# From the first layer to attention in one list of steps, with the query latent's inverse root moved into the exponential

## The chip, the cores and the metric

The kernel runs on one core of a Trainium2 chip. The metric is device microseconds of one execution, lower is better. Times of the profile are from one execution under the hardware profiler.

## The reference

Two layers over 1024 tokens of width 1024, all in 32-bit floats. Layer 0 is a short gated convolution and a squared-ReLU MLP. After it a shared key and value side is built from the residual stream, and layer 1 is attention over it, with an MLP. What concerns the change:

```python
hkv = modulate(rmsnorm(x, kv_norm_g), shift, scale)
kv_a = hkv @ kv_a_w                                    # 256 latent columns, 64 rotary ones
c_kv = rmsnorm(kv_a[..., :KV_LORA], kv_a_norm_g)
k_pe = apply_rope(kv_a[..., KV_LORA:], cos, sin)
kv = (c_kv @ kv_b_w).reshape(B, S, N_HEADS, QK_NOPE + V_HEAD)
...
q = (rmsnorm(h @ q_a_w, q_a_norm_g) @ q_b_w).reshape(B, S, N_HEADS, QK_NOPE + QK_ROPE)
# 8 heads; 384 latent columns; q_nope (128 wide) and rotated q_pe (64), both times 1/sqrt(192)
s = q_nope . k_nope + q_pe . k_pe;  masked block-causally in chunks of 64
p = softmax(s);  o = p @ v
```

## The kernel before

Each product of two matrices is made of three TensorE matmuls (`mm`, L170): both operands are split into a high and a low part, and low x high, high x low and high x high are summed in PSUM. The high part is a copy on ScalarE (the engine rows name it ACT), the low part a subtraction on VectorE (DVE) of the high part from the source; for weights that is `split_w`, L173 and L174. Most of the 512-column matmuls of a trace are such products.

Tokens are held in 8 tiles of 128 rows, or in 2 halves of 512. A framework schedules the instructions on each engine; where the code says `pinned()`, the written order is kept as it stands. Tiles on chip come from pools with a fixed number of buffers: `mm` and `tp` are PSUM banks of 512 columns, `big` ones of 1024; two `big` ones exist. `raw_tile()` gives one of four buffers for data from memory, and the transfers into them are queued in order on SyncE (SP).

The **end of layer 0's MLP** makes 24 matmuls for each of the 8 token tiles. `Seam` follows each with the sum, a norm, the gated residual and the norm for what comes next: on VectorE L309, L315, L316, on ScalarE two passes with squares (L255), a root (L257), and the row that the transposes need (L295). `h_steps` makes transposed operands for half the tokens: a group of four 128x128 transposes for each of 8 column blocks (L484), a scaled copy on ScalarE (L486, `tt`), and the split on VectorE (L490, L491). `first_block` then makes the first three column blocks of the query latent for half 0, with those steps between.

`latent` does, for the query latent (3 blocks) and the key-value latent (2), for each half: a copy from PSUM (L1305), squares (L1306), a sum over partitions by a matmul with ones (L1309), a root (L1310), a reciprocal over 128x512 elements (L1311), the scaling (L1313), and the split (L1314, L1315). `rotary_keys` makes the rotary keys: four copies of 32 partitions on ScalarE (L1322), and products with a cosine table `ctab` and a sine table `stab` on VectorE (L1323 to L1325).

**Attention** starts with `queries` (L1424, L1425), `rotary` and `keys` (L1418, L1419) of head 0, for half 1 and then half 0. Each head works through 8 score tiles from the longest (1024 keys) to the shortest: `scores` makes the matmuls into a `big` buffer (L1465), sets the masked corner (L1466), takes the negated maximum (L1468), the exponential with that maximum as bias and a running sum (L1471), and, as `end`, the reciprocal and the normalisation (L1475, L1476). `turn` transposes the weights p (L1491) and splits them (L1494, L1495), and the products with the values follow. Values of two heads at a time are made by `values` (L1448, L1449). Between them stand background tasks, sums of conditioning weights on VectorE (L195), whose weights come by 512 KB transfers. `load_q_b` and `load_kv_b` fetch the weights of the next heads.

Of the kernel before, what the change touches and what calls it, by code (L numbers as in the profile page):

```python
# [12 lines left out]
ALU = mybir.AluOpType  # L13
# [20 lines left out]
MASKED = -(2.0 ** 127)  # L34
# [17 lines left out]
P5_3 p6_0 nt2d p4_1 p3_2 D9_3 nS2 p6_3 nS3 p7_3 ns2a o6 p4_3 nt3a ns2d p5_3 nt3d o5 o4 p3_3 o3 o7  # L52
""".split()
# [8 lines left out]
def trunk_kernel(ctx: ExitStack, tc: tile.TileContext, x, c, ada_w, ada_b, norm_g, conv_in_w, conv_w,  # L62
# [95 lines left out]
    nc.vector.memset(eps_1, EPS)  # L158
    nc.scalar.activation(small(), eps_1, AF.Sqrt)
# [315 lines left out]
    def h_steps(tp, ys, half, key, dst):  # L475

        hi, lo = dst
        s1, sh = vtile["s" + key], vtile["h" + key]
        tts = {}

        def step(k):
            p_ = tp_ps()
            for t in range(4):
                nc.tensor.transpose(p_[:, t * P:(t + 1) * P], ys[half * 4 + t][:, k * P:(k + 1) * P], ident)  # L484
            tt = tp.tile([P, HALF], F32, tag="tt", name=nm("tt"), bufs=2)
            nc.scalar.activation(tt, p_, AF.Identity, scale=s1[:, k:k + 1], bias=sh[:, k:k + 1])  # L486
            tts[k] = tt

        def split(k):
            nc.vector.tensor_copy(hi[:, k, :], tts[k])  # L490
            nc.vector.tensor_tensor(lo[:, k, :], tts[k], hi[:, k, :].bitcast(F32), op=ALU.subtract)  # L491

        return [(lambda k=k: step(k), lambda k=k: split(k)) for k in range(KD)]

# [130 lines left out]

    def first_block(seam, steps0, steps1, ws, h):

        ps_ = [mm_ps(), mm_ps(), big_ps()[:, :HALF]]
        for k in range(KD):
            with pinned():  # L630
                for p_, w in zip(ps_, ws):
                    mm(p_, (w[0][:, k, :], w[1][:, k, :]), (h[0][:, k, :], h[1][:, k, :]), k == 0, k == KD - 1)
                if k == 0:
                    seam.back()
                    seam.front(steps0, 2)
                    seam.flush()
                elif k == 1:
                    seam.back()
                elif k >= 4:
                    seam.back()  # L640
                    seam.front(steps1, 2)
        with pinned():
            seam.back()
        return ps_
# [647 lines left out]
    def halves_of(*tiles):  # L1292
        return [t_[:, i * HALF:(i + 1) * HALF] for t_ in tiles for i in range(2)]
# [376 lines left out]
```

## Time and profile before

| | |
|---|---|
| time, median of 3 runs | 2152.4 us (2151.09 to 2154.95) |
| profiled execution | 2151.04 us, span 2149.3 us |
| TensorE busy (PE) | 2083.8 us, 97% |
| its weight loads (PEld) | 1712.5 us, 80% |
| VectorE (DVE) | 1530.3 us, 71% |
| ScalarE (ACT) | 1060.0 us, 49% |

The span is what the trace covers of the execution; a few microseconds lie around it. A row of the timeline gives start, duration, engine, line, operation, output and input, and in brackets the idle time ahead of it with what ended it. A row of the groups gives busy microseconds and mean nanoseconds of one, then the idle time ahead. A row of the windows gives for a stretch its length, the busy time of PE, PEld, DVE, ACT and POOL with counts, the granted TensorE clock, the share of the DMA engines, and GB/s.

### The profile page before, as it was taken

How to read it: one execution, taken by the hardware profiler on the slowest of the kernel's cores; microseconds unless marked ns; L12 is line 12 of the kernel's file. 1: busy time of each engine (PE TensorE's matmuls, PEld its weight loads, DVE VectorE, ACT ScalarE, POOL GpSimd, SP SyncE). 2: the span in 40 equal slices, each digit the busy share in tenths (PEclk: the TensorE clock that was granted, in tenths of full speed). 3: DMA queues.
4: the chain of work that ended last, by engine and by line, in shares of the span. 5: the costliest groups of instructions: out<-in, count | busy, mean ns of one | idle time of the engine just before them, and what ended most of it. 6: DMA issues, size and time to landing. Idle time of an engine off the chain costs nothing.

```text
span 2149.3 us, 25252 instructions
## 1 busy us (share of the span) xinstructions
PE 2083.8 (97%) x9638; PEld 1712.5 (80%) x9638; DVE 1530.3 (71%) x2063; ACT 1060.0 (49%) x1512; POOL 4.0 (0%) x8
## 2 busy tenths in 40 slices
PE   6999999999999999999899999999999999999998
PEld 5888888888888778888677888877888887788887
DVE  5877776977665677956788877765976665558556
ACT  4633354845454534344665555564845543444342
POOL 0000000000000000000000000000000000000000
PEclk9999999999999999999999999999999999999999
DMA  8344464466443976444214231043455543853243
GB/s 244 99 145 143 136 205 135 131 200 210 152 144 127 324 268 240 167 147 167 86 55 129 78 107 42 25 162 126 132 187 186 172 162 130 293 191 125 98 147 137
DMA packets 242335, 330.85 MB, mean 154 GB/s; under 512 B 18629, under 2 KB 143906, under 8 KB 242214
## 3 DMA queue, kind: packets, MB, share of 16 engines
q1 hardware_dynamic: 204328, 248.57, 36.6%
q10 hardware_dynamic: 37886, 80.67, 9.9%
q8 instruction: 76, 1.25, 0.2%
q14 instruction: 45, 0.37, 0.1%
HBM read 248.45 MB, written 80.74 MB: 153 GB/s over the span
## 4 chain that ended last, share of the span: by engine, by line
PE 73%; DVE 12%; ACT 7%; DMA 5%; issue 2%; SPq 0%; ACTq 0%; DVEq 0%
PE one L170 38%; PE mm L170 19%; PE tp L170 6%; PE big L170 4%; ACT junk L255 2%; DMA raw<-in_ada_w_dram 2%; PE big L1465 2%; DVE y L315 1%; DVE raw L316 1%; DVE acc L195 1%; PE tp L1491 1%; DMA raw<-in_kv_ada_w_dram 1%; DVE ring L174 1%; ACT small L257 1%; DVE y L309 1%
## 5 line engine op out<-in xcount | busy, mean ns | idle before, releaser
L170 PE MATMUL one<-slot,uphi 128*128 128x512 f32 x1240 | 382.0, 389 | 0.0
L170 PEld LDWEIGHTS one<-slot,uphi 128*128 128x128 f32 x1240 | 232.8, 188 | 48.5 <-issue 0.5
L170 PE MATMUL big<-slot 128*128 128x512 f32 x1152 | 265.6, 390 | 1.1 <-DVE slot L174 0.6
L170 PEld LDWEIGHTS big<-slot 128*128 128x128 f32 x1152 | 215.3, 188 | 47.0 <-DVE y L919 1.1
L170 PE MATMUL one<-slot,uplo 128*128 128x512 f32 x620 | 243.5, 393 | 3.6 <-ACT y L581 2.1
L170 PE MATMUL one<-ring,ring 128*128 128x512 f32 x1008 | 232.3, 391 | 6.2 <-DVE ring L174 6.1
L173 ACT ACTIVATE ring<-w 128x1024 fp32r<-128x1024 f32 x98 | 103.7, 1058 | 263.5 <-PE tp L170 134.0
L170 PEld LDWEIGHTS one<-ring,ring 128*128 128x128 f32 x1008 | 188.2, 188 | 49.2 <-ACT ring L173 5.6
L174 DVE TENSOR_TENSOR ring<-w,ring 128x1024 fp32r<-128x1024 f32 x98 | 119.9, 1223 | 111.5 <-ACT ring L173 111.5
L174 DVE TENSOR_TENSOR uplo<-raw,uphi 128x1024 fp32r<-128x1024 f32 x117 | 142.8, 1223 | 79.0 <-ACT uphi L173 78.9
L173 ACT ACTIVATE uphi<-raw 128x1024 fp32r<-128x1024 f32 x117 | 123.7, 1059 | 135.6 <-PE one L170 76.9
L170 PE MATMUL mm<-ring,ring 128*128 128x512 f32 x672 | 162.7, 390 | 1.0 <-DVE ring L174 1.0
L170 PE MATMUL tp<-ring,ring 128*128 128x512 f32 x672 | 161.7, 389 | 0.0
L170 PE MATMUL mm<-slot,uphi 128*128 128x512 f32 x504 | 158.3, 395 | 0.4 <-DVE slot L430 0.4
L170 PEld LDWEIGHTS mm<-ring,ring 128*128 128x128 f32 x672 | 125.6, 188 | 28.5 <-DVE ring L174 2.0
L170 PEld LDWEIGHTS tp<-ring,ring 128*128 128x128 f32 x672 | 126.1, 188 | 26.2
L195 DVE SCALAR_TENSOR_TENSOR acc<-raw,csil,acc 128x1024 f32<-128x1024 f32 x88 | 112.6, 1279 | 40.3 <-DMA raw<-in_ada_w_dram 36.0
L170 PEld LDWEIGHTS one<-slot,uplo 128*128 128x128 f32 x620 | 116.4, 188 | 30.3 <-ACT y L581 3.8
L174 DVE TENSOR_TENSOR ring<-raw,ring 128x1024 fp32r<-128x1024 f32 x98 | 119.6, 1220 | 18.1 <-ACT ring L173 18.1
L170 PE MATMUL one<-slot,s 128*128 128x512 f32 x468 | 112.6, 389 | 0.6 <-DVE s L174 0.6
L170 PEld LDWEIGHTS mm<-slot,uphi 128*128 128x128 f32 x504 | 94.8, 189 | 21.1 <-issue 1.4
L581 ACT ACTIVATE y<-one 128x512 f32<-128x512 f32 x62 | 36.7, 592 | 142.8 <-PE one L170 98.5
(271 smaller groups left out, 3486.5 us busy)
## 6 DMA issues: line engine op xcount, KB each, us to landing
ha<-y ACTq DMA_DIRECT2D x196, 256.0 KB, 3.0
raw<-ha SPq DMA_DIRECT2D x98, 512.0 KB, 4.1
raw<-in_ada_w_dram SPq DMA_DIRECT2D x80, 512.0 KB, 4.4
raw<-in_mlp_up_w_dram SPq DMA_DIRECT2D x70, 512.0 KB, 5.0
w<-in_mlp_down_w_dram SPq DMA_DIRECT2D x56, 512.0 KB, 4.9
raw<-hd SPq DMA_DIRECT2D x24, 512.0 KB, 4.5
xs<-raw ACTq DMA_DIRECT2D x24, 512.0 KB, 3.0
raw<-xs SPq DMA_DIRECT2D x24, 512.0 KB, 4.1
```

Source lines behind the costliest of these rows:

```text
L170: nc.tensor.matmul(out_, lhs[a], rhs[b], start=first and i == 0, stop=last and i == 2, skip_group_check=more)
L173: nc.scalar.activation(hi, src, AF.Copy)
L174: nc.vector.tensor_tensor(lo, src, hi.bitcast(F32), op=ALU.subtract)
L195: nc.vector.scalar_tensor_tensor(acc, raw, s, acc, op0=ALU.mult, op1=ALU.add)
L255: nc.scalar.activation(junk, src, AF.Square, accum_out=ss)
L257: nc.scalar.activation(rt, ss, AF.Sqrt, bias=eps_d)
L309: nc.vector.tensor_tensor(y, y, p_, op=ALU.add)
L315: nc.vector.scalar_tensor_tensor(y, y, rroot(ss), self.gmb, op0=ALU.mult, op1=ALU.mult)
L316: nc.vector.tensor_tensor(xr, xr, y, op=ALU.add)
L581: nc.scalar.activation(dst, x_, AF.Copy)
L1465: nc.tensor.matmul(o_, a, m_, start=j == 0, stop=j == 4)
L1491: nc.tensor.transpose(p_[:, c:c + P], pts[4 * hf + i][:, j * P:(j + 1) * P], ident)
```

## The change

There are three parts.

1. A list of step names, `LATENTS`, replaces `h_steps`, `first_block`, `latent` and `rotary_keys`. From token tile 5 on, everything from the MLP's end to the last kv latent is written in that order, all pinned. Its names: `mm5` products of tile 5; `tr0_2`, `tu0_2`, `sp0_2` transposes, scaled copy and split of column block 2 for the queries' half 0 (`k0`, `k1` for the keys'); `f0` to `f7` and `g0` to `g3`, `e0` to `e2` the query latent's products; `qh`, `ql`, `qq` its high part, low part and squares; `qs`, `qr`, `qi` sums, root and inverse; `v..` the same for the kv latent; `k..` the rotary keys; `wa`, `wd` the split of the kv weights.
2. The query latent is not normalised any more. Its parts are taken from PSUM with the gain as the only factor. The sum of squares goes, by four matmuls of one column for each half, into a table `rsq` of 128x8, one column for each query tile, with the softmax's 1/sqrt(192) folded in. Each score tile multiplies its negated maximum by its column (one 128x1 operation on VectorE), and the exponential takes it as its scale. The mask's value becomes -2^120.
3. At attention's start the order becomes queries and rotary of half 1, keys of half 0, values 0 and 1, queries and rotary of half 0, keys of half 1. Values 2 stand after score tile 7, values 3 after tile 6 (both stood after 6 before). Five background tasks a head are called in heads 1 to 6 in place of 0 to 5.

```diff
-MASKED = -(2.0 ** 127)
+MASKED = -(2.0 ** 120)
+LATENTS = """
+mm5 tr0_0 mm6 tu0_0 add5 sp0_0 sq5 rc4 pre4 stt5 tr0_1 xad5 tr0_2 tu0_1 mm7 add6 dma5 tu0_2 sp0_1 sqx5 sp0_2 sq6 rc5
...
+vh11 vh10 vl11 vl10 ks1 kh1 kl1
+""".split()
...
-        down(slots, sizes, wd, src_fn, ys, seam, steps0, 0, lambda: ws.extend(up_weights(up, [w]) for w in wcols), begun)
+        down(slots, sizes, wd, src_fn, ys, seam, None, 0, lambda: ws.extend(up_weights(up, [w]) for w in wcols), begun)
...
-            nc.scalar.activation(raws[m], p_, AF.Copy)
-            nc.scalar.activation(sqs[min(m, 1)], raws[m], AF.Square)
...
-        nc.tensor.matmul(sp, ones, sqs[0], start=True, stop=True)
-        nc.scalar.activation(rs, sp, AF.Sqrt, scale=1.0 / (n * P), bias=eps_1)
-        nc.vector.reciprocal(rs, rs)
-        for m in range(n):
-            nc.vector.scalar_tensor_tensor(raws[m], raws[m], g[:, m:m + 1], rs, op0=ALU.mult, op1=ALU.mult)
-            nc.scalar.activation(dst[0][:, m, sl], raws[m], AF.Copy)
...
+        def q_high(hf, m):
+            nc.scalar.activation(qaT[0][:, m, half(hf)], out_[hf][m], AF.Copy, scale=gq[:, m:m + 1])
...
+        def q_sums(hf):
+            p_ = t_["qs", hf] = big_ps() if hf else mm_ps()
+            for t in range(4):
+                nc.tensor.matmul(p_[:, t:t + 1], t_["sq", hf][0][:, t * P:(t + 1) * P], ones[:, 0:1], start=True, stop=True)
...
+        def q_root(hf):
+            nc.scalar.activation(rsq[:, 4 * hf:4 * hf + 4], t_["qs", hf][:, :4], AF.Sqrt, scale=(NOPE + ROPE) / QL, bias=eps_q)
...
+        with pinned():
+            for name in LATENTS:
+                acts[name]()
...
+        rs = rsq[:, i:i + 1]
+        nc.vector.tensor_tensor(mx, mx, rs, op=ALU.mult)
...
-        nc.scalar.activation(pt, sp[:, :n], AF.Exp, bias=mx, accum_out=l_)
+        nc.scalar.activation(pt, sp[:, :n], AF.Exp, scale=rs, bias=mx, accum_out=l_)
...
-    for hf in (1, 0):
-        queries(Q, qw_, hf)
-        rotary(R, qw_, hf, tp_ps)
-        keys(K, kw, 0, hf)
+    queries(Q, qw_, 1)
+    rotary(R, qw_, 1, tp_ps)
+    keys(K, kw, 0, 0)
+    for b in range(2):
+        values(V, kw, b)
+    queries(Q, qw_, 0)
+    rotary(R, qw_, 0, tp_ps)
+    keys(K, kw, 0, 1)
...
-        run_bg(5)
+        run_bg(5 if h else 0)
...
-            values(V, kw0, 0)
-            values(V, kw0, 1)
+            values(V, kw0, 2)
...
-            values(V, kw0, 2)
             values(V, kw0, 3)
```

How the instructions stand on the engines, in three places. First TensorE at the end of the MLP. Each run of four rows with `big` is one token tile's products; `tp` is a group of transposes and `y` a tile's row. Before:

```order
L170 MATMUL big_7479<-slot_7214 128x512 x6
L484 MATMUL tp_7515<-cs,y_5382 128x128
L484 MATMUL tp_7515<-cs,y_5383 128x128
L484 MATMUL tp_7515<-cs,y_5384 128x128
L170 MATMUL big_7539<-slot_6957 128x512 x6
L170 MATMUL big_7539<-slot_6958 128x512 x6
L170 MATMUL big_7539<-slot_6959 128x512 x6
L170 MATMUL big_7539<-slot_7214 128x512
L484 MATMUL tp_7515<-cs,y_5385 128x128
```

And in the changed kernel:

```order
L187 MATMUL big_7507<-slot_7217 128x512 x6
L1318 MATMUL tp_7532<-cs,y_5385 128x128
L1318 MATMUL tp_7532<-cs,y_5386 128x128
L1318 MATMUL tp_7532<-cs,y_5387 128x128
L1318 MATMUL tp_7532<-cs,y_5388 128x128
L187 MATMUL big_7537<-slot_6960 128x512 x6
L187 MATMUL big_7537<-slot_6961 128x512 x6
```

The fourth transpose of the first group, the one of tile 3's row, stood after 19 of the 24 products of tile 6 and now stands ahead of them all.

Second, ScalarE at the start of attention. `kw` is the high part of the kv weights for heads 2 and 3, `z` the rotary copies of the queries, `k` the keys, `r` the rotated queries, `v` the values. Before:

```order
L1322 ACTIVATE z_8376<-tp_8377 32x512 x4
L1348 ACTIVATE slot_6957<-y_8314 128x512
L1418 ACTIVATE k_8407<-mm_8400 128x512
L1424 ACTIVATE q_8421<-mm_8411 128x512
L1434 ACTIVATE r_8394<-z_8375 64x512
L1434 ACTIVATE r_8395<-z_8375 64x512
L1322 ACTIVATE z_8426<-tp_8427 32x512 x4
L1418 ACTIVATE k_8457<-mm_8450 128x512
L1448 ACTIVATE v_8510<-mm_8497 128x512
L1434 ACTIVATE r_8444<-z_8425 64x512
L1434 ACTIVATE r_8445<-z_8425 64x512
L173 ACTIVATE kw_8953<-raw_8831 128x1024
```

And in the changed kernel:

```order
L1534 ACTIVATE q_8362<-mm_8352 128x512
L190 ACTIVATE kw_8937<-raw_8813 128x1024
L1269 ACTIVATE z_8367<-tp_8368 32x512 x4
L1528 ACTIVATE k_8398<-mm_8391 128x512
L1422 ACTIVATE ckT_7227<-y_8255 128x512 x2
L1558 ACTIVATE v_8415<-mm_8402 128x512
L1445 ACTIVATE slot_6960<-y_8322 128x512
L1544 ACTIVATE r_8385<-z_8366 64x512
```

`kw`, which stood behind the rotary copies, keys and r's of both halves, now stands ahead of those of the first.

Third, VectorE in head 0's score tiles. `small` with `big` as its source is a tile's maximum, `p` the exponentials, `acc` a background task. Before:

```order
L1475 RECIPROCAL small_8529<-small_8495 128x1
L1468 TENSOR_REDUCE small_8544<-big_8532 128x1
L1476 TENSOR_SCALAR p_8494<-p_8494,small_8529 128x1024
L1449 TENSOR_TENSOR v_8562<-mm_8549,v_8562 128x512
L1449 TENSOR_TENSOR v_8578<-mm_8565,v_8578 128x512
```

And in the changed kernel:

```order
L1587 RECIPROCAL small_8520<-small_8502 128x1
L1578 TENSOR_REDUCE small_8535<-big_8523 128x1
L1588 TENSOR_SCALAR p_8501<-p_8501,small_8520 128x1024
L1580 TENSOR_TENSOR small_8535<-small_8535,rsq 128x1
L1576 MEMSET big_8560 64x64
```

The new 128x1 product stands behind the normalisation of the tile before, and the exponential needs it; before, the exponential needed the maximum alone.

More of the change, by code (lines that the diff above doesn't have):

```diff
@@ L473, in quarter_steps @@
         return acts
[L475 to L493, printed above, removed]
     def up_weights(up, cols, kk=KD):
@@ L624, in up_mm @@
         return p_
[L626 to L644, printed above, removed]
     def first_pairs(seam, acts, up, wmat, ws, ops):
```

231 lines of the change are left out of this document (171 added, 60 removed).

## The prediction

> **What bounds the kernel now.** I read the page first, then windows of 25 us over the stretch that the change rewrites (1010 to 1165 us), then TensorE's timeline there with its waits, and last the rows that price single operations.
>
> ```profile
> span 2149.3 us, 25252 instructions
> PE 2083.8 (97%) x9638; PEld 1712.5 (80%) x9638; DVE 1530.3 (71%) x2063; ACT 1060.0 (49%) x1512; POOL 4.0 (0%) x8
> PE 73%; DVE 12%; ACT 7%; DMA 5%; issue 2%; SPq 0%; ACTq 0%; DVEq 0%
> ```
>
> TensorE is busy for 97% of the span. Only 2149.3 - 2083.8 = 65 us are there to be won by order alone. The windows (columns: PE busy, PEld, DVE, ACT, POOL, then granted TensorE clock) show that the stretch holds some of them:
>
> ```profile
> 1025.00:1050.00 25.00, 20.50 (x100) 16.21 (x99) 18.90 (x32) 16.34 (x27) 0.00 (x0) 0.93 0.32 106
> 1050.00:1075.00 25.00, 22.85 (x116) 18.20 (x115) 20.05 (x29) 16.08 (x25) 0.00 (x0) 1.00 0.22 62
> 1075.00:1100.00 25.00, 25.00 (x130) 19.43 (x129) 21.19 (x33) 14.96 (x23) 0.00 (x0) 1.00 0.10 26
> 1125.00:1150.00 25.00, 21.05 (x112) 16.90 (x111) 24.30 (x37) 16.58 (x27) 0.00 (x0) 1.00 0.58 180
> ```
>
> Idle are 4.50 us at the end of the MLP (and the clock falls), 2.15 after it, nothing in the middle, 3.95 where attention starts; there VectorE is full (24.30 of 25). The timeline of TensorE names the waits in brackets:
>
> ```profile
> 1031.18 1.33 PE L484 MATMUL tp<-cs,y 128*128 128x128 f32 x8 [3.41 <-ACT tt L486]
> 1056.22 0.48 PE L170 MATMUL mm<-slot,uplo 128*128 128x512 f32 x1
> 1070.66 0.50 PE L170 MATMUL mm<-slot,uplo 128*128 128x512 f32 x1 [2.03 <-ACT lat L1305]
> 1071.46 0.60 PE L484 MATMUL tp<-cs,y 128*128 128x128 f32 x4
> 1071.82 0.47 PE L170 MATMUL mm<-slot,uplo 128*128 128x512 f32 x1
> 1120.25 2.20 PE L170 MATMUL mm<-slot,w 128*128 128x512 f32 x9
> 1122.29 2.20 PE L170 MATMUL tp<-slot,w 128*128 128x512 f32 x9
> 1157.38 1.09 PE L1491 MATMUL tp<-cs,p 128*128 128x128 f32 x8 [0.37 <-DVE p L1476]
> 1158.72 0.50 PE L170 MATMUL mm<-pt,v 128*128 128x512 f32 x1 [0.25 <-ACT pt L1494]
> ...
> 1028.00:1031.00 3.00, 0.00 (x0) 0.00 (x0) 2.90 (x7) 2.85 (x5) 0.00 (x0) 1.00 0.23 91
> 1033.00:1036.00 3.00, 3.00 (x8) 2.04 (x7) 2.90 (x8) 2.82 (x7) 0.00 (x0) 0.53 0.75 265
> ```
>
> Nine matmuls take 1122.29 - 1120.25 = 2.04 us, 0.227 each. After the idle 3.41 us the clock fell to 0.53 and the nine of the next block took 3.9, so 1.85 more; after the idle 2.03 (in the window from 1050) it stayed at 1.00. A group of four transposes takes 1071.82 - 1071.46 = 0.36.
>
> **The change part by part.** First, the end of the MLP. In the new order TensorE's tile 6 stands behind the first whole group of four transposes, and the fourth of them needs tile 3's row, which ScalarE writes here:
>
> ```profile
> 1017.05 1.14 ACT L295 ACTIVATE y<-raw,small 128x1024 f32<-128x1024 f32 x1
> 1014.30 1.06 ACT L255 ACTIVATE junk<-raw 128x1024 bf16<-128x1024 f32 x1 [2.14 <-DVE raw L316]
> 1020.32 1.06 ACT L255 ACTIVATE junk<-raw 128x1024 bf16<-128x1024 f32 x1 [2.14 <-DVE raw L316]
> 1014.63 0.49 PE L484 MATMUL tp<-cs,y 128*128 128x128 f32 x3
> ```
>
> The row is there at 1018.2; the first three, which need older rows, are done by about 1015.0 (1014.63 and 0.36). So a new wait of 3.2 us arises. It costs little as such: ScalarE and VectorE pass a tile in 1020.32 - 1014.30 = 6.02 us, TensorE needs 24 x 0.227 = 5.45, so it must wait for them in any case. Walking on, two tiles at 5.45 and two transpose groups bring the last product to about 1030.0; eight blocks of 2.04, five transpose groups (0.36) and one wait, about 1.35 by the same rows, for the last operand that VectorE splits end at 1050.4; seven groups of the next half, which the kernel before does among its blocks, make it 1052.9. The same work stands at 1056.22 now: **-3.3 us**. The new wait of 3.2 lies between 2.03 (clock kept) and 3.41 (clock lost) and nearer to the latter, so I charge the lost clock: 1.85, of which two tiles' slack of 0.57 each takes 1.15, so +0.7. **-2.6** in all; bounds -3.3, and 0 if the wait is only moved.
>
> The Trainium skill ("TensorE: Matmul & The Clock Gate", section "HAM oscillation — how this bites in real kernels") gives about 3.4 us of idleness, a free-running window, as what halves the clock. By that 3.2 would not do it and this term would be 0.7 lower; that an idle 3.41, just one window long, did it here says that the edge is not sharp, so the row stands.
>
> Second, the q latent. Its normalisation leaves the way (the wait of 2.03 hangs on it), and two sums over partitions change their form:
>
> ```profile
> L1309 PE MATMUL tp<-sq,ones 128*128 128x512 f32 x8 | 4.5, 641 | 0.2
> L214 PE MATMUL one<-ones,acc 128*128 128x1 f32 x32 | 3.7, 245 | 0.0
> L1311 DVE RECIPROCAL sq<-sq 128x512 f32<-128x512 f32 x4 | 13.4, 3351 | 5.9 <-ACT sq L1310 5.9
> ```
>
> Eight records for four sums are 2 x 0.641 = 1.28 us for each; four columns of one are about 4 x 0.23. Two sums: 2 x (1.28 - 0.92) = 0.7 saved; the wait of 2.03 goes, since queries' raw sums now go from PSUM straight to operands. Two reciprocals of 3.35 leave VectorE, which had no wait of TensorE under them in the full window (1075 to 1100), so they pay nothing themselves. **-2.7 us**; -0.7 if another wait takes that one's place. So the first query product (1120.25) starts 5.3 earlier, at T = 1114.9.
>
> Third, the start of attention. ScalarE's high part of the kv weights for heads 2 and 3 now stands ahead of the rotary copies of the first half. Before, it stood behind the second pair of r's and waited for nothing:
>
> ```profile
> 1132.63 1.44 SPq L127 DMA_DIRECT2D raw<-in_q_b_w_dram  x3
> 1135.38 0.37 SPq L127 DMA_DIRECT2D raw<-in_kv_b_w_dram  x1
> 1139.10 1.06 ACT L173 ACTIVATE kw<-raw 128x1024 fp32r<-128x1024 f32 x1
> 1125.23 2.39 ACT L1322 ACTIVATE z<-tp 32x512 f32<-32x512 f32 x4
> 1128.31 0.60 ACT L1418 ACTIVATE k<-mm 128x512 fp32r<-128x512 f32 x1
> 1128.92 0.68 DVE L1324 TENSOR_TENSOR z<-z,stab 128x512 f32<-128x512 f32 x1
> 1129.53 0.68 DVE L1419 TENSOR_TENSOR k<-mm,k 128x512 fp32r<-128x512 f32 x1
> raw<-in_q_b_w_dram SPq DMA_DIRECT2D x4, 192.0 KB, 2.6
> ```
>
> Its transfer is on SP's queue behind three for q weights, whose buffer was the sine table's until VectorE's last multiplication with it. That one ends at about T + 2.5 (four copies of 2.39 in all after the rotary key product, then two VectorE operations). The q requests take 1.44, so the kv request goes at T + 3.9 at the earliest; landing takes between 2.6 (the smaller q transfer) and 3.72 (1139.10 - 1135.38), I take 3.2: T + 7.1. ScalarE gets there at T + 3.0 (the key product is done one sum over partitions, 1.2, before T, its four copies end at T + 1.2, then come three operations of some 0.6) and stands for 4.1 us. Behind it in its queue: 1.06 for itself, four rotary copies (2.39), keys' copy (0.60), two halves of the kv latent (about 0.60 each); behind those on VectorE the rotary product, two low halves, an addition, the sine product and the keys' low part, at 0.61 each (1129.53 - 1128.92): T + 14.8. For that one TensorE's second block of values waits, as it reuses keys' PSUM buffer; TensorE is there after 33 x 0.227 + 12 x 0.12 = 8.9. It waits **5.9 us**. Carried on by the same rows: values, now ahead of the scores, no longer lie under the softmax, so score tiles 4, 3 and 2 wait 1.4, 1.6 and 1.8 us for an exponential, and the last score block before the transposes ends at T + 40.9. Now that is 1157.38 - 1120.25 = 37.13. **+3.8 us**; without the blocked queue it would be -0.1, the lower bound, and the 2.3 us by which the rows of before exceed products plus waits could come on top: +6.1. An idle 5.9 loses the clock (3.41 did): 1.85, of which the two short waits right behind it (0.4 and 0.9) hide 1.3: **+0.5**. Next, score tile 1 waits about 1.15 where the wait at 1158.72 is 0.25: **+0.9**.
>
> Fourth, every score tile gets one more VectorE operation of 128x1 between the maximum and the exponential, and the exponential reads one more operand of one value per partition:
>
> ```profile
> L219 DVE TENSOR_TENSOR v<-v,vecs 128x8 f32<-128x8 f32 x4 | 0.6, 158 | 0.0
> L1476 DVE TENSOR_SCALAR p<-p,small 128x640 f32<-128x640 f32 x7 | 3.9, 552 | 0.2
> L1305 ACT ACTIVATE lat<-mm 128x512 f32<-128x512 f32 x8 | 4.5, 594 | 2.5 <-DVE ckT L1315 1.2 <-PE mm L170 0.7 <-DVE slot L1315 0.6
> L486 ACT ACTIVATE tt<-tp,v,v 128x512 f32<-128x512 f32 x32 | 23.9, 774 | 12.0 <-PE tp L484 11.0 <-DVE slot L491 0.6 <-PE mm L170 0.3
> PE tp L1491 <- DVE p L1476: 1.2, 4, 0.3
> PE big L1465 <- ACT p L1471: 1.1, 2, 0.7
> ```
>
> The operation is bounded by the nearest row, 0.16 us for 128x8 (0.15 taken). A copy from PSUM takes 594 ns, one with two such operands 774, so each is 0.09. So 0.24 us more per tile, 64 times; VectorE, busy for 71% of the span, has room for 64 x 0.15 = 9.6. In addition the order puts an operation between the maximum and the new one in most tiles, in half of them the normalisation of the tile before, 0.55 by the middle row; together about 0.7. What hides this: two score tiles have PSUM room, and TensorE has the last head's transposes and products to do meanwhile. The waits of TensorE on this chain in heads 1 to 7 (1165 to 1410 us, the last two rows: us, times, longest) are six, and each grows by 0.24 at least: **+1.4 us**; with the other operation in each, 6 x 0.7 = 4.2; nothing, if slack elsewhere takes it. The plain folds (scale of 1/sqrt(192), the mask's value, the sine table) exchange operations of equal length: nothing, under VectorE's other work. Of the five running sums of conditioning weights that move from head 0 to head 6, head 0's VectorE keeps as many in the new order, and head 6 has VectorE time free: nothing; without that cover five operations of at most twice the 0.68 of a row half as wide, 6.8.
>
> Sum: -2.6 - 2.7 + 3.8 + 0.5 + 0.9 + 1.4 = **+1.3 us**. The profiled execution took 2151.04 (span 2149.3), so 2152.3 in its terms; the runs' median is 2152.4, 1.4 above it, so I forecast **2153.7 us**. A measurement of this kernel can tell about 0.2%, 4.3 us, from no change: I forecast no change.
>
> **The rivals.** *The transfer comes in time, and the softmax stays covered.* For it: 3.2 us for landing and the request's time are my bounds' middle, and in heads 1 to 7 TensorE waits for this chain six times only. Then the 5.9 shrinks by the blocked 4.1 less 0.2, the clock holds, and score tile 1 and the heads lose nothing: 2153.7 - 3.9 - 0.5 - 0.9 - 1.4 = 2147.0, faster. Against it: SP's queue is in order, and the sine buffer's release fixes the request.
>
> *The softmax chain comes out from under TensorE's work* and the kernel is slower. Place: score tiles of all heads, TensorE's wait for the exponential. Price 0.7 per exposed tile, 56 tiles in heads 1 to 7. It decides from the point where a quarter of them is exposed: 14 x 0.7 = 9.8, less the 1.4 counted: 2153.7 + 8.4 = 2162.1. For it: half of the tiles wait behind a normalisation. Against it: only six waits on the chain there now, none above 0.7.
>
> *The change doesn't do what it says at the MLP's end:* the wait of 3.41 is only moved to the first transpose group and delays all behind it. The first term is 0 instead of -2.6: 2156.3. For it: the new wait is nearly as long. Against it: ScalarE and VectorE set the pace there.
>
> **How the numbers follow.** Forecast 0.43, transfer in time 0.36, softmax exposed 0.16, wait moved 0.05. The forecast's own spread (its bounds on the sums, some 3 us either way, 2150 to 2158) puts 0.04 of it on faster, 0.70 on same, 0.26 on slower. The second case is faster in three of four, the third slower in nearly all, the last half same, half slower. Faster 0.017 + 0.27 = 0.29; same 0.30 + 0.09 + 0.02 = 0.41; slower 0.11 + 0.16 + 0.03 = 0.30. The range reaches just past the two outer cases' prices, 2146 to 2162.
>
> **What would show it.** Right: in the new profile the first transpose group carries a wait near 3.2 and the idle 2.03 for the latent's copy is gone; the first query product starts near 1115; ScalarE's high part for kv waits some 4 us for its transfer there, and TensorE stands near 6 us before the second values block, with the clock at half after it. Wrong: if that copy waits for no transfer, the second case holds; if heads 1 to 7 show TensorE waiting on exponentials more than some ten times, the third; if the first query product does not start before 1119, the last. The forecast as a whole is wrong outside 2148.1 to 2156.7.

## The result and the profile after

The changed kernel takes 2166.53 us (median of four runs, 2163.71 to 2169.63) against 2151.9 for the kernel before beside it: ratio 1.0066, interval [1.005, 1.0082]. By the ratio it is slower by 14.2 us, and its time lies outside the range of 2146 to 2162. Its profiled execution has a span 14.5 us longer. From its page, the span, the busy time of the engines, and the chain's shares:

```profile
span 2163.8 us, 25317 instructions
PE 2097.1 (97%) x9650; PEld 1716.8 (79%) x9650; DVE 1523.2 (70%) x2122; ACT 1061.8 (49%) x1506; POOL 4.0 (0%) x8
PE 80%; DVE 8%; ACT 6%; DMA 4%; issue 1%; ACTq 0%; SPq 0%; DVEq 0%
```

TensorE is busy 13.3 us longer (2083.8 before) though its records count only twelve matmuls more. Nearly the whole loss looks like work, not like waiting; that is the first thing to explain. Its windows over the rewritten stretch (the columns are those of the prediction):

```profile
1025.00:1050.00 25.00, 25.00 (x126) 20.93 (x125) 18.50 (x32) 19.70 (x34) 0.00 (x0) 0.98 0.63 188
1050.00:1075.00 25.00, 25.00 (x136) 20.90 (x136) 15.90 (x29) 13.80 (x21) 0.00 (x0) 1.00 0.01 3
1075.00:1100.00 25.00, 23.39 (x131) 19.78 (x130) 20.55 (x37) 16.54 (x26) 0.95 (x1) 1.00 0.16 46
1125.00:1150.00 25.00, 22.33 (x118) 18.09 (x117) 24.65 (x36) 16.96 (x28) 0.00 (x0) 1.00 0.29 88
```

TensorE's idle time there is 1.6 us in the third window and 2.7 in the last; the 4.5 and 2.15 of the kernel before in the first two are gone (a new wait of 3.04 stands just ahead of them, in the rows below). To see where time goes I cut the execution at four places that both kernels have: the first transposes behind the MLP's tile 5, the first query product, the first and the last transposes of p, and TensorE's end. Rows of TensorE's timeline, changed kernel:

```profile
1018.92 0.49 PE L1318 MATMUL tp<-cs,y 128*128 128x128 f32 x3
1022.45 0.48 PE L1318 MATMUL tp<-cs,y 128*128 128x128 f32 x1 [3.04 <-ACT y L312]
1120.40 2.62 PE L187 MATMUL mm<-slot,w 128*128 128x512 f32 x9
1159.36 0.88 PE L1603 MATMUL tp<-cs,p 128*128 128x128 f32 x6
1431.63 0.38 PE L1603 MATMUL tp<-cs,p 128*128 128x128 f32 x2
2129.68 26.52 PE L187 MATMUL big<-slot 128*128 128x512 f32 x115
```

And the two places of the kernel before that the prediction doesn't show (the others are 1014.63, 1120.25 and 1157.38 there):

```profile
1420.89 0.38 PE L1491 MATMUL tp<-cs,p 128*128 128x128 f32 x2
2129.70 11.95 PE L170 MATMUL big<-slot 128*128 128x512 f32 x52
```

| stage, us | before | after | difference | predicted |
|---|---|---|---|---|
| start to the MLP's end | 1014.63 | 1018.92 | +4.3 | 0 |
| passage, to the first query product | 105.62 | 101.48 | -4.1 | -5.3 |
| attention's start, to the first transposes of p | 37.13 | 38.96 | +1.8 | +4.3 |
| heads, to the last transposes of p | 263.51 | 272.27 | +8.8 | +2.3 |
| rest (layer 1's MLP) | 720.76 | 724.57 | +3.8 | 0 |

The first and last rows are code that the change doesn't touch, but for tile 5's products, with which the list begins; they give 8.1 of the 14.5. The heads give 8.8. TensorE's waits in the heads (1165 to 1420 us; engine and tile waiting, what it waits for, us, times, longest), changed kernel:

```profile
PE big L1575 <- ACT p L1583: 6.8, 8, 2.3
PE mm L187 <- DVE pt L1607: 2.3, 6, 0.5
PE mm L187 <- ACT pt L1606: 0.6, 3, 0.2
PE tp L1603 <- DVE p L1588: 0.3, 1, 0.3
```

The wait on exponentials was 1.1 us (the prediction's row) and is 6.8. The longest of them, first TensorE's row, then VectorE's rows before it, then two windows of TensorE's clock around it (the clock is the third number from the end), all of the changed kernel:

```profile
1234.51 0.69 PE L1575 MATMUL big<-slot,r 128*128 128x384 f32 x1 [2.33 <-ACT p L1583]
```

```profile
1230.78 1.28 DVE L212 SCALAR_TENSOR_TENSOR acc<-raw,csil,acc 128x1024 f32<-128x1024 f32 x1 [1.09 <-DMA raw<-in_ada_w_dram]
1231.98 0.16 DVE L1587 RECIPROCAL small<-small 128x1 f32<-128x1 f32 x1
1232.05 0.81 DVE L1578 TENSOR_REDUCE small<-big 128x1 f32<-128x640 f32 x1
1232.77 0.61 DVE L1588 TENSOR_SCALAR p<-p,small 128x768 f32<-128x768 f32 x1
1233.30 0.15 DVE L1580 TENSOR_TENSOR small<-small,rsq 128x1 f32<-128x1 f32 x1
```

```profile
1232.00:1234.50 2.50, 0.18 (x1) 0.00 (x0) 2.17 (x8) 0.97 (x2) 0.00 (x0) 0.90 0.54 144
1234.50:1237.90 3.40, 3.39 (x15) 3.30 (x16) 2.59 (x7) 1.40 (x3) 0.00 (x0) 0.57 0.12 48
```

A background sum stands 1.09 us for its transfer and 1.28 for itself, ahead of a maximum; a normalisation stands between the maximum and the new product; the exponential can start only at the end of that. Then the clock is at 0.57 for 3.4 us, in the mean of a window that reaches a little past the end of the slow stretch; from 1234.25 to 1237.25 it is 0.50.

### The profile page after: what moved, and what is told of

The parts are those of the page before. It is cut to its first block, busy times and chain, and to the rows that moved or that the text cites. A ratio compares the mean times of both kernels' runs of the same rounds, so it can differ in the third digit from the quotient of the medians.

```text
span 2163.8 us, 25317 instructions
## 1 busy us (share of the span) xinstructions
PE 2097.1 (97%) x9650; PEld 1716.8 (79%) x9650; DVE 1523.2 (70%) x2122; ACT 1061.8 (49%) x1506; POOL 4.0 (0%) x8
## 4 chain that ended last, share of the span: by engine, by line
PE 80%; DVE 8%; ACT 6%; DMA 4%; issue 1%; ACTq 0%; SPq 0%; DVEq 0%
PE one L187 41%; PE mm L187 19%; PE big L187 8%; PE tp L187 7%; PE big L1575 2%; ACT junk L272 2%; DMA raw<-in_ada_w_dram 1%; DVE y L332 1%; PE tp L1603 1%; DVE raw L333 1%; DVE acc L212 1%; ACT z L1269 1%; DMA raw<-ha 1%; PE tp L1318 1%; DVE small L1578 1%
## 5 line engine op out<-in xcount | busy, mean ns | idle before, releaser
L187 PE MATMUL mm<-slot,uphi 128*128 128x512 f32 x424 | 131.9, 392 | 0.4 <-DVE slot L447 0.4
L190 ACT ACTIVATE ring<-raw 128x1024 fp32r<-128x1024 f32 x98 | 102.2, 1045 | 7.5 <-DMA raw<-ha 7.5
```

Of the source, the lines that this page charges most:

```text
L187: nc.tensor.matmul(out_, lhs[a], rhs[b], start=first and i == 0, stop=last and i == 2, skip_group_check=more)
L190: nc.scalar.activation(hi, src, AF.Copy)
```

## The experiments

Each kernel ran four to twelve times, with the kernel before beside it; effects are the ratios to it, times 2152 us. "Heads" and "rest" are the stages of the table above, read in the same way from each kernel's one profiled execution; a stretch of half clock, which some of these executions have there and others not, makes the heads some 1.7 us longer, so small differences in that column say little. In the two kernels without the scale (e8, e10) the query latent's inverse root is applied nowhere, so their times are those of less work.

| kernel | ratio, interval | effect, us | heads | rest |
|---|---|---|---|---|
| before | 1 | 0 | 263.5 | 720.8 |
| after | 1.0066 [1.005, 1.0082] | +14.2 | 272.3 | 724.6 |
| e2: before, 64 bytes of padding | 1.0041 [1.0027, 1.0055] | +8.8 | 265.3 | 723.9 |
| e5: before, padded at both ends | 1.0041 [1.0027, 1.0055] | +8.8 | 263.7 | 723.3 |
| e9: before, 256 bytes of padding | 0.9998 [0.9988, 1.0008] | -0.4 | 263.6 | 719.9 |
| e1: after, 64 bytes more | 1.0075 [1.0062, 1.0087] | +16.1 | 274.6 | 723.9 |
| e6: after at the old addresses | 1.0039 [1.0027, 1.0051] | +8.4 | 274.1 | 721.0 |
| e19: e6, background sums in heads 0 to 5 | 1.0008 [0.9998, 1.0017] | +1.7 | 268.1 | 720.6 |
| e7: e6, attention's start as before | 1.0012 [1.0002, 1.0022] | +2.6 | 268.0 | 720.7 |
| e8: e6 without the scale | 0.9983 [0.9974, 0.9993] | -3.7 | 263.7 | 719.8 |
| e10: e7 without the scale | 0.9987 [0.9979, 0.9996] | -2.8 | 264.5 | 720.2 |
| e11: before, product and scale | 1.004 [1.0027, 1.0052] | +8.6 | 269.1 | 721.3 |
| e14: before, scale alone | 0.9995 [0.9987, 1.0004] | -1.1 | 265.0 | 719.9 |
| e15: before, product alone | 1.0024 [1.0016, 1.0033] | +5.2 | 269.5 | 719.8 |

**Addresses.** The change brings two small new tables, which take 64 bytes of each partition. Everything that is allocated after them from that end lies 64 bytes higher, part of the slots that hold the matmuls' moving operands among them, and all of `q`; the weights, allocated from the other end, stay. In groups of TensorE by line and operands (busy us, mean ns of one), kernel before, then changed:

```profile
L170 PE MATMUL one<-slot,uplo 128*128 128x512 f32 x620 | 243.5, 393 | 3.6 <-ACT y L581 2.1 <-DVE y L583 1.6
```

```profile
L187 PE MATMUL one<-slot,uplo 128*128 128x512 f32 x620 | 246.1, 397 | 3.6 <-ACT y L578 2.1 <-DVE y L580 1.6
```

The same 620 matmuls became 4 ns longer each. The 1008 with both operands in `ring`, tiles at the other end, keep their mean of 391. Five kernels test that.

```diff
 e2 (before), e1 (after): +     cp.tile([P, 16], F32, name="pad")
 e9 (before):             +     cp.tile([P, 64], F32, name="pad")
 e5 (before): e2's line, and as many bytes at the other end
              +     padr = pool("padr", "right")
              +     padr.tile([P, 16], F32, name="padr")
 e6 (after): the table in the place of an unused tile, the constant beside another
-    cp.tile([P, 8], F32, name="even")
+    rsq = cp.tile([P, NT], F32, name="rsq")
-    eps_1 = cp.tile([P, 1], F32, name="eps_1")
+    eps_ = cp.tile([P, 2], F32, name="eps_1")
+    eps_1, eps_q = eps_[:, 0:1], eps_[:, 1:2]
```

> The changed kernel with one more unused tile of 64 bytes per partition behind the two small new ones, so that everything on the left side of SBUF lies 128 bytes further than in the kernel before, not 64; the instructions and their order are the same. Theory A (addresses): the shift by 64 bytes makes matmuls slow whose one operand lies on the left side and whose other lies on the right; then the untouched stretch up to 1000 us loses its 4.2 us and the last 700 us their 3.4, the mean distance of one<-slot,uplo matmuls goes back to 227 ns, and the time is about 2166 - 9 = 2157 us. Theory B (the whole loss lies in the changed stretch, and the rest of the shift is chance or another chip): no change, 2166 us. Theory C (softmax chain alone): no change either.

> The kernel before with an unused tile of 64 bytes per partition where the change puts its two small tiles; the instructions and their order are the same as before. Theory A (addresses): slower by 8 to 10 us, 2161 us, with matmuls of slot and uplo at 230 ns or more and those of ring and ring at 227. Theories B and C: no change, 2152 us.

> The kernel before with 64 unused bytes per partition on the left side and 64 on the right side of SBUF, so that the two operands of each matmul keep their distance modulo 128 bytes and both lie 64 bytes off. If the relative place of the two operands decides, no change: 2152 us, ring and slot matmuls at 227 ns. If the place of each alone decides, slower than with the left pad, as ring and uphi move too: 2165 us or more. Theories B and C: 2152 us.

> The changed kernel with its two small new tiles put into room that the kernel before already had (rsq into an unused tile of 32 bytes, the second constant beside the first), so that every large tile has the address it had before; the instructions and their order are those of the changed kernel. Theory A (addresses): the left pad alone cost the kernel before 8.6 us, so this is faster than the changed kernel by 8 to 10 us, near 2157.5 us, with slot and uplo matmuls at 227 ns, and the rest, some 5.5 us over the kernel before, is the new order and the scaled exponential. Rival (the changed stretch itself reacts to nothing of this and the addresses cost it nothing): 2162 us.

> The kernel before with 256 unused bytes per partition on the left side, in place of 64. If what counts is the distance between the two operands modulo 256 bytes (it is a multiple of 512 in the kernel before, 51712 between the first slot and the first uphi), no change: 2152 us and 227 ns. If modulo 512 or more, 2158 to 2162 us and 229 ns or more for slot and uphi.

Sixty-four unused bytes cost the kernel before 8.8 us, with not one instruction changed. Its group is the changed kernel's:

```profile
L171 PE MATMUL one<-slot,uplo 128*128 128x512 f32 x620 | 246.1, 397 | 3.6 <-ACT y L582 2.1 <-DVE y L584 1.6
```

With 256 bytes it is back (ratio 0.9998):

```profile
L171 PE MATMUL one<-slot,uplo 128*128 128x512 f32 x620 | 243.3, 392 | 3.6 <-ACT y L582 2.1 <-DVE y L584 1.6
```

Since e5 changes the distance of the two ends by 128 and costs the same 8.8, and e1 stands at 128 too and gains nothing, my idea that 128 bytes would restore it fell. Changes of the distance by 64 and 128 bytes cost and one of 256 doesn't. That the distance counts, and not the address of the moving operand alone, is seen in a group that tells 64 from 128. In e2 and e5 the moving operand lies at the same address, in e1 64 bytes further; e1 and e5 have the same distance. Rows of e2, e5 and e1 (389 ns in the kernel before):

```profile
L171 PE MATMUL one<-q,uphi 128*128 128x512 f32 x328 | 101.6, 391 | 0.0
L173 PE MATMUL one<-q,uphi 128*128 128x512 f32 x328 | 102.9, 395 | 0.0
L188 PE MATMUL one<-q,uphi 128*128 128x512 f32 x328 | 102.9, 395 | 0.0
```

The two of one distance agree. In e5 the operands in `ring` move together by 64 bytes, and their mean stays at 391. Back at the old addresses the changed kernel (e6) is 5.8 us better by the ratios. Those intervals just touch, but the rest of the program settles the sign: that stage is 719.8 to 721.3 us in every kernel at the old distance (and in e9) and 723.3 to 724.6 in every one off it. The first stage agrees: where tile 6 stands behind the first transposes it ends at 1013.8 to 1016.9 us at the old distance and at 1018.3 to 1020.5 off it.

**The scale and the start, together and apart.**

```diff
 e7 (from e6): attention's start, and its background sums, as before
 e4 (from e1): the same, on the shifted addresses
 e8 (from e6), e10 (from e7):
-        nc.vector.tensor_tensor(mx, mx, rs, op=ALU.mult)
-        nc.scalar.activation(pt, sp[:, :n], AF.Exp, scale=rs, bias=mx, accum_out=l_)
+        nc.scalar.activation(pt, sp[:, :n], AF.Exp, bias=mx, accum_out=l_)
 e11 (from before):
+        rs = ones[:, i:i + 1]
+        nc.vector.tensor_tensor(mx, mx, rs, op=ALU.mult)
-        nc.scalar.activation(pt, sp[:, :n], AF.Exp, bias=mx, accum_out=l_)
+        nc.scalar.activation(pt, sp[:, :n], AF.Exp, scale=rs, bias=mx, accum_out=l_)
```

> The padded changed kernel with the start of attention in the order of before (queries, rotary, keys for half 1, then half 0; values behind the scores; background tasks from head 0 on); the step list and the scale in the exponential stay. By the prediction's third term the new start costs 3.8 + 0.5 + 0.9 us against the old one, so this is 5 us faster than the padded changed kernel. Rival: the start gained or lost nothing, since the first transposes of p came 2.0 us later while the shift ahead was 4.2, so it is within 2 us of it or slower.

> The changed kernel at the old addresses and with the start of attention in the order of before; step list and scaled exponential stay. In the padded pair the old start gained 4.3 us (2163.55 against 2167.84). If the new start costs what the prediction's third term says (5 us with its clock and the wait after it), 2153 us here; if the gain in the padded pair came from addresses, no gain here: 2157.5 us.

> The changed kernel at the old addresses without the 128x1 product on the maximum and without the scale in the exponential; the inverse root, and 1/sqrt(192) with it, is then not applied at all, so the weights are those of another softmax. If the longer chain before the exponential is what heads 1 to 7 lose (8.7 us between 1159 and 1415 us in the changed kernel, with 8 waits of TensorE for an exponential where there were 2), this is faster than the changed kernel at the old addresses by 5 to 8 us. By the prediction's size for it, 1.4 us faster. If those waits come from something else, no change.

> The changed kernel at the old addresses, with the old start of attention and without the product on the maximum and the scale in the exponential (the inverse root is not applied at all). What is left of the change is the step list and the latent's missing normalisation. Theory (the three parts add up): 2155.0 - 13.0 = 2142 us, so the passage alone gains 10 us against the kernel before. Rival (the scale costs 13 us only with the new start, which leaves the exponentials of head 0 uncovered): 2149 to 2153 us.

> The kernel before, at its own addresses, with the 128x1 product on each maximum and a scale operand in each exponential, both by a column of ones; nothing else. Theory (each of the 64 score tiles pays the longer chain nearly in full): 64 x 0.2 = 13 us, 2165 us. The prediction's size: 0.24 us at six waits, 1.4 us, 2154 us. Rival (the scale costs much only beside the new step list): within 4 us of the kernel before.

The list and the raw latent alone (e10) gain 2.8 us. The scale costs 5.4 on top with the old start (e10 to e7) and 12.1 with the new one (e8 to e6); in the kernel before it costs 8.6. The new start costs 5.8 with the scale (e7 to e6) and -0.9 without (e10 to e8). On shifted addresses the old start gained as well: e4 1.0052 [1.0039, 1.0065], heads 269.1, against e1, though these two intervals overlap a little. So the new start, which costs nothing without the scale, costs beside it.

**What of the scale costs.** The product was taken apart from the longer exponential (e14, e15), the normalisations were held behind the product (e13), and the product was given to ScalarE (e16) and GpSimd (e17).

```diff
 e14 (from before): scale=ones[:, i:i + 1] in the exponential, no product
 e15 (from before): the product with ones, no scale
 e13 (from e7): maximum, product, then the normalisation of the tile before, kept in this order
 e16, e17 (from e12, below)
-        nc.vector.tensor_tensor(mx, mx, rs, op=ALU.mult)
+        nc.scalar.activation(mx, mx, AF.Copy, scale=rs)          # e16
+        nc.gpsimd.tensor_tensor(mx, mx, rs, op=ALU.mult)         # e17
```

> The changed kernel at the old addresses and with the old start of attention; on VectorE the maximum, the product on it and then the normalisation of the tile before are held in this order, so that 28 of 64 products stand right behind their maximum (or a memset) where 5 did, and 6 behind a normalisation where 30 or more did. If the operation that stands between is what the scale costs, 4 to 8 us faster than 2155.0. If the product and the operand themselves are (0.24 us a tile), no change or slightly slower, since the normalisations wait longer.

> The kernel before, with the exponential reading its scale from a column of ones; no product on the maximum. Theory A (each part of the chain maximum, product, exponential costs by its own length, wherever it stands): the exponential is 0.10 us longer in each of 64 tiles, so up to 6.4 us, and by the 8.2 that both together cost, about 3.3, so 2154.6. Theory B (the product costs by its place behind a normalisation in VectorE's queue, the longer exponential is covered): within 1 us of before. Theory C (the exponential's length is what counts, since the two buffers of scores are released by it): 6 to 8 us slower, 2158 to 2160.

> The kernel before, with the negated maximum multiplied by a column of ones on VectorE; the exponential as it was. Theory A: 0.15 us for each of 64 tiles by the same share, about 4.9 us slower, 2156.2. Theory B: 7 to 8 us slower. Theory C: within 2 us of before.

> The list, the un-normalised latent and the scale, with the order of attention's start and of the seam's first transposes as before and the two new tables at addresses that leave the others in place; the product on the maximum is made on ScalarE, right ahead of the exponential, and no longer stands in VectorE's queue. With it on VectorE the same kernel stood at 1.0006 [0.9997, 1.0014]. Theory B (place in VectorE's queue): most of the scale's 6.1 us comes back less the copy's own length, about 2148, faster than before. Theory A: the copy costs ScalarE about 0.2 us a tile where the product cost VectorE 0.15, so no better: 2152 to 2154. Theory C: the product costs nothing in either place, so 2152.

> The same with the product on GpSimd, an engine that has nothing else to do in attention. The product then waits for no other work, but two passages between engines come in place of one. Theory B: between the two, 2149 to 2152 if a passage costs no more than the queue did. Theory A: its own length and the second passage, at least 0.2 us more a tile, so over 2155.

The longer exponential is covered, the product is not. Groups of ScalarE, kernel before, then e14:

```profile
L1471 ACT ACTIVATE p<-big,small 128x1024 f32<-128x1024 f32 (+3 forms) x64 | 47.4, 740 | 37.3 <-DVE small L1468 36.9
```

```profile
L1471 ACT ACTIVATE p<-big,small,ones 128x1024 f32<-128x1024 f32 (+3 forms) x64 | 53.2, 832 | 38.5 <-DVE small L1468 38.1
```

Each exponential takes 92 ns more in e14, and the kernel is no slower. e15 leaves the exponential alone and costs 5.2. ScalarE's waits ahead of its exponentials (1125 to 1425 us) show the chain's length; kernel before, then e15:

```profile
ACT p L1471 <- DVE small L1468: 36.9, 29, 2.2
```

```profile
ACT p L1472 <- DVE small L1471: 44.3, 42, 2.1
```

In e14 they are 38.1 us in 30. With the product 29 waits became 42, and their sum grew by 7.4 us for 64 products of 0.15. Whether the length or the engine of the product counts is asked by e16 (0.9991 [0.9983, 1.0]) and e17. From e16's groups, the product on ScalarE; then its waits ahead of it:

```profile
L1579 ACT ACTIVATE small<-small,rsq 128x1 f32<-128x1 f32 x64 | 18.8, 294 | 34.0 <-DVE small L1577 33.5
```

```profile
ACT small L1579 <- DVE small L1577: 33.5, 34, 1.9
```

At 294 ns it is twice as long as on VectorE (151), and the kernel goes from 1.0006 (e12) to 0.9991, the heads from 267.8 to 266.4: at most a small gain, as the intervals overlap. On GpSimd (e17, 1.0017 [1.0008, 1.0026], heads 270.5) it is 266 ns and the heads are longer than on either. Between e16 and e17 the intervals are apart, with nearly equal lengths: the engine counts, and the length alone does not decide. That the product on VectorE costs by its place in the queue is not shown by this, since e16 and e12 are not told apart. e13 is a miss of mine: 1.0055 [1.0043, 1.0067], heads 275.9. With the product right behind its maximum TensorE waited longer on exponentials (1125 to 1425 us) than in any other kernel:

```profile
PE big L1574 <- ACT p L1585: 15.4, 9, 3.3
```

So it is not borne out that the product costs by the normalisation that stands ahead of it. Why this order is worse stays open: the edit puts the normalisations, which the transposes need, behind one maximum more, but the transposes' waits for them are no longer than in e7 (1.3 us against 2.1, 1165 to 1420 us).

**What meets what at the new start.**

```diff
 e19 (from e6):
-        run_bg(5 if h else 0)
+        run_bg(5)
 e18 (from e6): the product on ScalarE as in e16, tile 6 ahead of the transposes as in e12
```

> The changed kernel with three edits: the two new tables at addresses that leave the others in place, tile 6's products ahead of the seam's first transposes as before, and the product on the maximum on ScalarE. Attention's new start stays. If the new start and the scale meet through the product in VectorE's queue (the new start moves five background sums into heads 1 to 6, and one of them stands waiting for its transfer ahead of a maximum), the start costs no more here than the -1.0 us that it showed without the scale: 2149 to 2151, level with or below the kernel with the old start and the product on ScalarE (2150.8). If they meet because the values no longer cover head 0's score tiles, whatever engine makes the product, some 5 us stay: 2155 to 2157.

> The changed kernel at the old addresses (2160.9), with the background sums back in heads 0 to 5. If their new place (heads 1 to 6) makes the 5.9 us, since one of them waits 1.1 to 1.5 us for its transfer ahead of a maximum and TensorE then waits 2.3 to 2.7 and loses clock, this comes to 2155 to 2157. If head 0 is what lacks cover, five more sums there make it worse: 2161 to 2165.

e19 settles which part of the new start costs: with the new order of queries, keys and values, but the background sums back in heads 0 to 5, the kernel is at 1.0008, level with the old start, and 6.7 us better than e6. The row of e6 at the place shown above, on TensorE's timeline, and that of e19:

```profile
1231.93 0.69 PE L1574 MATMUL big<-slot,r 128*128 128x384 f32 x1 [2.69 <-ACT p L1582]
```

```profile
1229.17 0.44 PE L1574 MATMUL big<-slot,r 128*128 128x384 f32 x1 [0.42 <-ACT p L1582]
```

The order of attention's start costs nothing; the sums' new heads cost, beside the product. What they cost in the traces is waiting and clock. TensorE in the heads of e6, then of e19, and last e6 behind the wait above (length, busy time, and the clock third from the end):

```profile
1155.93:1430.07 274.14, 259.74 (x1435) 215.91 (x1436) 208.47 (x482) 153.95 (x300) 0.00 (x0) 0.98 0.23 71
1156.31:1424.40 268.09, 256.42 (x1436) 212.33 (x1436) 204.51 (x479) 154.29 (x300) 0.00 (x0) 1.00 0.21 64
1230.75:1237.25 6.50, 5.32 (x20) 5.11 (x21) 5.10 (x14) 3.04 (x6) 0.00 (x0) 0.50 0.34 103
```

Of the 6.1 us by which e6's heads are longer, TensorE is idle for 2.7 (14.4 against 11.7) and busy for 3.3, for nearly the same matmuls; e6 has half clock for the 6.5 us shown and for some 3.4 at 1425, e19 nowhere in its heads. How the sums' place makes the exponentials late is not settled. A sum's wait for its transfer can't be all of it, since VectorE's sums wait longer for transfers in e19 than in e6 (1165 to 1420 us: 3.5 us in three waits, 2.0 the longest, against 2.0 in three, 1.5 the longest); what differs for certain is where the sums stand. Nor is the product in VectorE's queue all of it: e18 (1.0008 [0.9999, 1.0017]) lies between its two expectations, and with the product on ScalarE start and sums cost 3.7 against e16, whose interval it just touches.

**The passage.**

```diff
 e12 (from e7):
-mm5 tr0_0 mm6 tu0_0 add5
+mm5 mm6 tr0_0 tu0_0 add5
```

> The changed kernel at the old addresses and with the old start of attention, its list altered in one place: the first group of four transposes stands behind tile 6's products, not ahead of them. If ScalarE and VectorE set the pace there, as the prediction has it, the wait of 3.0 us and the clock lost after it were covered: within 1 us of 2155.0. If TensorE sets it: 3 to 5 us faster, 2151 us.

e12 is at 1.0006 [0.9997, 1.0014], e7 at 1.0012: not told apart. Its median is 3.1 us lower, but the kernels before beside them differ by 1.1, and from tile 5's first product, placed by the mean spacing of the products, to the first query product both need about 106 us. The wait of 3.04 that the new order makes costs nothing that I could measure.

## Why the prediction was wrong

The steps, by ratio, from the kernel before to the changed one: list and raw latent -2.8 (e10), scale +5.4 (e7), order of attention's start -0.9 (e19), sums moved +6.7 (e6), addresses +5.8 (after): 14.2.

**The addresses: a step that was missing.** The prediction took code that isn't touched to keep its time and gave no reason; that is 8.1 of the 14.5 by the stages in one execution, 5.8 by e6. A hint stood in the program, not in the profile: the kernel before holds a 32-byte tile that nothing uses and that sets the addresses behind it.

**The heads: sized at 1.4 (with 0.9 for score tile 1), 8.8 in the trace.** The prediction laid the price on the six waits that the trace of before shows and took the rest for covered. By the runs the scale costs 5.4 (e10 to e7), and in e15 the product alone costs 5.2 and makes the heads 6.0 longer. The rival that named this mechanism, the softmax chain exposed, had 0.16 and 2162.1; its sign for that (more than some ten waits on exponentials) was not reached, with eight. Waits are not the whole of it. TensorE between the same two places, kernel before, then changed:

```profile
1157.38:1420.89 263.51, 254.84 (x1435) 212.28 (x1436) 203.95 (x421) 147.92 (x300) 0.00 (x0) 1.00 0.21 68
1159.36:1431.63 272.27, 258.70 (x1435) 214.05 (x1436) 208.10 (x482) 153.90 (x300) 0.00 (x0) 0.99 0.23 70
```

It is idle for 13.6 us in place of 8.7, 4.9 more, and busy for 3.9 more with as many matmuls. The clock's stretch at 0.57 shown above costs 3.4 x 0.43 = 1.5 and a second one (0.51, last section) 1.7, so 3.2 of the 3.9. Clock lost with a wait is a price that the prediction's 0.24 for each wait left out. The addresses add little there: e5's heads are 0.2 longer, and the 1.8 of e2 hold a slow stretch (0.57 from 1422.5 to 1426.5 us, 1.7).

**The moved sums: costed at nothing, measured 6.7.** The step asked whether VectorE has time in head 6, for the sums alone. Without the scale the new start costs nothing with them (e8 against e10); beside it they lengthen TensorE's waits on exponentials, and the clock falls behind the longest. That the two would meet was in none of the terms.

**The blocked copy: did not happen.** ScalarE's and TensorE's timeline and SyncE's request, changed kernel:

```profile
1106.56 0.37 SPq L141 DMA_DIRECT2D raw<-in_kv_b_w_dram  x1
1124.03 1.06 ACT L190 ACTIVATE kw<-raw 128x1024 fp32r<-128x1024 f32 x1
1132.64 1.70 PE L187 MATMUL mm<-w,ckT 128*128 128x256 f32 x12 [2.31 <-DVE k L1529]
1152.34 0.50 PE L1575 MATMUL big<-slot,r 128*128 128x512 f32 x1 [1.26 <-ACT p L1583]
1155.27 0.50 PE L1575 MATMUL big<-slot,r 128*128 128x512 f32 x1 [1.01 <-ACT p L1583]
1158.11 0.44 PE L1575 MATMUL big<-slot,r 128*128 128x384 f32 x1 [1.41 <-ACT p L1583]
```

The request went 13.8 us ahead of the first query product, where the step had it 3.9 behind: it did not wait for the sine table's last use. So the copy had no wait, and TensorE stood 2.31 us for the keys instead of 5.9. The three waits for exponentials behind it were predicted at 1.4, 1.6 and 1.8 and are 1.26, 1.01 and 1.41. The rival that forecast this, the transfer in time, had 0.36; its 2147.0 failed by the other steps. The stage cost 1.8 instead of 4.3, and not by the new start: with that start and no scale it takes 37.3 us (e8), with the old one and the product alone 38.7 (e15), against 37.1 before.

**What held.** The wait at the first transposes (3.04 for 3.2) with the clock lost after it, as this window of the changed kernel shows:

```profile
1022.50:1025.50 3.00, 3.00 (x8) 2.42 (x9) 2.73 (x3) 0.96 (x1) 0.00 (x0) 0.50 0.63 213
```

Further the end of the wait of 2.03 for the latent, though two waits of 1.20 and 0.41 on scaled copies stand at 1077 us instead; and the passage, 4.1 shorter for 5.3. Its first term rests on a slip: 1030.0 and the eight blocks (16.3), five transpose groups (1.8) and one wait (1.35) make 1049.5, not 1050.4, so it should have been 0.9 larger. In the same way six VectorE operations of 0.61 behind the blocked copy would end at T + 16.0, not 14.8, if all of them stand behind ScalarE's last. The small -2.8 of e10, in which the inverse root is left out, is all that the list and the raw latent bring to the whole.

## What to carry to other kernels

A new small table is a change of every address behind it: pad the old kernel by as many bytes before any reason is sought in the new order. One more short operation on a chain between two engines can cost far more than its length times the waits that the old trace shows, as a longer wait can cost clock too: try it alone in the old kernel, as e15 does, and try it on the engine that needs its result, which was no worse here at twice the length. And an edit that costs nothing by itself can cost 7 us beside another, so parts are to be tried together as well as apart.

## What was not expected of the hardware

The distance of a matmul's two operands in on-chip memory changes its time in this kernel: 393 to 397 ns in the mean for one group at 64 bytes more, 389 to 395 for another at 128; 8.8 us of 2152 for the kernel at either, and nothing at 256. The mechanism is open.

The clock fell with shorter waits than the 3.41 of the kernel before: to 0.57 with an idle 2.33; and, in the windows of the changed kernel below, to 0.51 after sixteen one-column products, in which TensorE counts as busy:

```profile
1292.00:1295.40 3.40, 3.15 (x26) 2.76 (x25) 1.33 (x4) 0.60 (x1) 0.00 (x0) 1.00 0.24 96
1295.40:1298.80 3.40, 3.40 (x14) 2.92 (x13) 3.39 (x8) 1.19 (x2) 0.00 (x0) 0.51 0.49 148
```

It stayed at 1.00 after the idle 2.03 of the kernel before. The Trainium skill ("TensorE: Matmul & The Clock Gate", section "HAM oscillation — how this bites in real kernels") puts the limit at idleness above about 3.4 us; 2.33 and 3.04 did it here (and 2.69 in e6), so for single waits the measurement decides. Why the sixteen products are followed by it is not shown.
